# Reordering the first token-mixer stage of a two-layer diffusion backbone: an early PSUM copy, another order of gates, conditioning loads and norms

## The chip, the cores and the metric

The kernel runs on one core of one Trainium2 chip. The metric is the device time of one execution in microseconds, taken as the median of several runs. Engines are named as the profile names them: PE (TensorE, matrix products), DVE (VectorE), ACT (ScalarE), POOL (GpSimd) and SP (SyncE, which here only issues the DMA transfers). Each engine takes its own instructions in order, and waits on semaphores where it needs another engine's result.

## The reference

Two layers over 512 latent tokens of width 1024 and 256 context tokens. The first stage, which the change touches, is the pooling mixer of layer 0 up to the input of its MLP:

```python
sh1, sc1, gt1, sh2, sc2, gt2 = ada_mods(c, w_ada[i], b_ada[i])             # SiLU(c) @ w_ada + b_ada
csh1, csc1, cgt1, csh2, csc2, cgt2 = ada_mods(c_ctx, w_ada[i], b_ada[i])
h_lat = modulate(rms_norm(x, g_mix_pre[i]), sh1, sc1)                      # h * (1 + sc) + sh
h_ctx = modulate(rms_norm(ctx, g_mix_pre[i]), csh1, csc1)
y_lat = pool_mixer(h_lat, w_pool[j], pool_scale[j])
y_ctx = None if last else pool_mixer(h_ctx, w_pool[j], pool_scale[j])
x = x + gt1 * rms_norm(y_lat, g_mix_post[i])
m_lat = sq_relu_mlp(modulate(rms_norm(x, g_mlp_pre[i]), sh2, sc2), w_mlp_in[i], w_mlp_out[i])
x = x + gt2 * rms_norm(m_lat, g_mlp_post[i])
```

The context tokens take the same steps with their own vectors (`cgt1`, `csc2`, ...). Layer 1 is an attention layer with another MLP. All of it is float32; the large products are made from a high and a low part of each operand, three products for one.

## The kernel before

The 768 tokens are six tiles of 128 rows: tiles 0 to 3 are latent, 4 and 5 context. `xr` holds the residual stream, `acc` (seen as `accv[:, t, :]`) the tile that is being worked on, `hH`/`hL` (both in the buffer `ra`) the transposed input of the next product as high and low part, and `rb` the weights.

After the pooled means the stage runs, for each tile t in the order 4, 5, 0, 1, 2, 3:

- `pool_a`: 24 products of 128x256 columns into two PSUM banks (`pspool`). Tiles 4 and 5 do it early and in pieces; tile 4 has two small banks of the pool `psB` (four banks in all), the other tiles a double bank of `psA` (two double banks).
- `pool_ms`: the mean square of the mixer output, on ACT straight from PSUM (two activations with an accumulator, line 170), then two tiny POOL instructions (lines 183 and 185) that make the reciprocal root.
- `pool_b`: the mixer output times the gate row, on DVE, two halves of 512 columns (`gated`, line 326), into `acc`.
- `norm_r`: the residual add on DVE (line 329), `norm_s`: mean square of the new row on ACT and the root on POOL, `norm_c`: the scaled row into `acc`, on ACT (line 521) for every second tile and on DVE (line 523) for the others.

Then pairs of tiles (4,5), (0,1), (2,3) are transposed on PE, a quarter of the columns at a time (`turn0`, line 379, 4 transposes into `psx`), and modulated (`mod0`: two rows on ACT, line 389, and on DVE, line 391, and the split into high and low part, lines 395 and 396). The first MLP product (`Inner.part`, line 562) uses each quarter as soon as it is there.

The conditioning vectors come from 14 entries of `CONDITIONING`. Each is a load from `w_ada` (1 MB, or two for a wide entry), a small product `ada_mm` (line 227; 8 matmuls whose 32-column pieces lie side by side in the array), a DVE transpose (line 233), a small product with `sel` (line 238) and an add (line 249). The entries 6 and 7 are the mixer's gate GT1, 8 and 9 the MLP's scale SC2 and shift SH2 for the first half of the columns, 10 to 13 the same for the second half. A gate row is made from such a vector by `gate_rows` (4 matmuls into `psg`, a copy by ACT into `gate`), for latent tokens (`ci` 0) and context tokens (`ci` 1) and for two halves of the columns each.

The order of all this is a table of numbers: `st.at(z, function, ...)` enters a step at due time z, and the steps are emitted by rising z. Up to z = 47.3 (DVE and ACT) and 48 (PE) the emitted order is kept on each engine; in the rest of the stage a scheduler with a timing model of its own may reorder. Loads of `w_ada` go into four buffers in SBUF, so a load can be issued once the matmuls on the load four places ahead of it are done; all loads go through SP's one queue. The weights of the first MLP product are loaded once (`w_in(0, 0, ...)`) and split into `rb` by ACT (line 142) and DVE (line 145).

Of the kernel before, what the change touches and what calls it, by code (L numbers as in the profile page):

```python
# [22 lines left out]
TOK = LAT + CTX  # L23
# [11 lines left out]
SH1, SC1, GT1, SH2, SC2, GT2 = range(6)  # L35
# [33 lines left out]
def backbone(ctx: ExitStack, tc, x, ctx_in, w_ada, w_pool, pool_scale, w_qkv, g_q, g_k, w_o, w_mlp_in,  # L69
# [4 lines left out]
    te, ve, sc = Kept(tc, nc.tensor, ordered), Kept(tc, nc.vector, mixed), Kept(tc, nc.scalar, mixed)  # L74
# [42 lines left out]
    hH = ra[:, 0:KT * TOK].rearrange("p (k n) -> p k n", n=TOK)  # L117
    hL = ra[:, KT * TOK:].rearrange("p (k n) -> p k n", n=TOK)
    accv = acc.rearrange("p (t n) -> p t n", n=D)
# [19 lines left out]
    def split(raw, hi, lo, pin=False, q=None):  # L139
        if q is not None:  # L140
            raw, hi, lo = (z[:, 512 * q:512 * q + 512] for z in (raw, hi, lo))
        a = sc.copy(hi, raw)  # L142
        if pin:
            tc.keep_in_program_order(a)
        b = ve.tensor_tensor(out=lo, in0=raw, in1=hi, op=ALU.subtract)  # L145
        if pin:
            tc.keep_in_program_order(b)
# [177 lines left out]
    def gated(t, dst, src, n0, n1, pool=False):  # L325
        return (gp if pool else ve).tensor_tensor(out=dst[:, n0:n1], in0=src, in1=gate[:, slot[t], n0:n1], op=ALU.mult)
# [107 lines left out]
    rs, mix, yg, first = {}, {}, {}, []  # L434
# [62 lines left out]
            mean_square(pss[q], ss[:, q:q + 1])  # L497
        rs[t] = rstd(ss, 2)

    def pool_b(t):  # L500
        for q in range(2):
            gated(t, accv[:, t, :], mix[t][q], 512 * q, 512 * q + 512)

    def norm_r(t, half=False):
# [34 lines left out]
    hids0 = [(rb[:, 3072 * b:3072 * b + 1536], rb[:, 3072 * b + 1536:3072 * b + 3072]) for b in range(2)]  # L539
# [58 lines left out]
    ring = Ring(unit)  # L598
# [117 lines left out]
    def w_in(i, g, rg, pin=False, wait=None):  # L716
        return rg.load(w_mlp_in[i, g], 256, pin, wait)
# [4 lines left out]
    st = Steps()  # L722
    for t in range(NT):
        st.at(4.6 + 1.3 * t, rows_a, t)
    landing = ((19.3, 21.4, 22.4), (23.8, 25.9, 27), (27.1, 28.15, 28.7), (28.9, 30.0, 30.5), (31.4, 32.4, 33.4),
               (33.7, 34.8, 35.2), (40.6, 42.65, 43.9), (44.2, 46.25, 47.2),
               (51, 53, 53.8), (55.8, 57.8, 58.6), (60.5, 61.5, 62), (62.9, 63.9, 64.4), (65.2, 66.2, 66.7), (67.7, 68.7, 69.2))
    for zs, (m, j, w) in zip(landing, CONDITIONING):
        for z, fn, also in zip(zs, (ada_mm, ada_rows, ada_sel), ((w,), (), ())):
            st.at(z, fn, 0, m, j, *also)  # L730
# [27 lines left out]
        st.at((21.5, 23.4)[h], pool_split, h, True)  # L758
        st.at((23.4, 24.4)[h], pool_split, h, False)
    raws = []  # L760
    st.at(56.5, lambda: first.append(Inner(0, w_in(0, 0, ring, False, raws), hH, hL, hids0[0], chunks0, TOK)))
    st.at(58, lambda: split(*raws[0]))
    for h in range(2):
        for ci in range(2):
            st.at((46.2, 47.6)[h] + (0.1, 0)[ci], gate_rows, 0, GT1, ci, (h,))
    order = (4, 5, 0, 1, 2, 3)
    for z, t, g in ((30.6, 4, 0), (32.5, 4, 1), (35.4, 4, 2), (36.2, 5, 0), (36.3, 5, 1), (36.4, 5, 2), (42.6, 4, 3), (42.62, 5, 3)):
        st.at(z, pool_a, t, (g,), t == 4)
    for n, t in enumerate(order):
        b = 50.5 + 2.9 * n  # L770
        if n > 1:
            st.at((47.9, 52.6, 55.6, 58.4)[n - 2], pool_a, t)
        st.at((43.8, 44.6, 50.6, 55.6, 58.6, 61.4)[n], pool_ms, t)
        st.at(b, pool_b, t)
        st.at(b + 1.5, norm_r, t)
        st.at(b + 2.8, norm_s, t)
        st.at(b + 4, norm_c, t, n % 2 == 1)
    parts0 = lambda t, q, f: first[0].part(t, f, range(2 * q, 2 * q + 2))
    block = {(4, 0): 58, (4, 1): 59.4, (0, 0): 63.4, (0, 1): 64.7, (4, 2): 66, (0, 2): 67.3, (2, 0): 69, (2, 1): 70.2,
             (2, 2): 71.4, (4, 3): 72.6, (0, 3): 73.8, (2, 3): 75}  # L780
    for (t, q), z in block.items():
        st.at(z, turn0, t, q)
        st.at(z + 0.8, mod0, t, q)
        for f in range(2):
            st.at(z + 2.4 if q < 3 else 76.5 + 2 * f + t / 10, parts0, t, q, f)
    st.at(200, open_units)
    st.run()

# [663 lines left out]
```

## Time and profile before

| what | value |
|---|---|
| median of 3 runs | 1178.41 us (1176.73 to 1180.56) |
| the profiled execution | 1178.11 us |
| its span, first to last instruction | 1176.3 us |
| mean granted PE clock | 0.996 of full speed |
| DVE busy | 938.4 us (80%) |
| ACT busy | 635.0 us (54%) |
| POOL busy | 68.1 us (6%) |

The span is what the trace shows; the profiled execution's own time holds 1.8 us around it. A row of the timeline has its start, its length, engine, source line, operation, the tiles written and read, their shape and a count, and in brackets how long the engine stood idle before it and what ended that. Steps that keep the emitted order show the line of the recording helper, 65, in place of their own. A matmul of float32 counts twice in the timeline's count where it is made of two passes. Rows of the window view give busy time of PE, weight loads, DVE, ACT and POOL, then the granted PE clock, the share of DMA engines busy, and GB/s.

### The profile page before, as it was taken

What the parts mean: (1) busy time and instruction counts of PE and PEld (TensorE: products, weight loads), DVE (VectorE), ACT (ScalarE), POOL (GpSimd) and SP (SyncE); (2) the same over time, 40 slices, a digit from 0 to 9 for tenths busy, and PEclk for the clock granted to TensorE, in tenths of its full rate; (3) what the DMA queues carried; (4) which work ended last, traced back from release to release, by engine and by line L of the source; (5) the groups of instructions that cost most, each with busy time, mean ns of one, the idle gap of its engine ahead of it and who ended that gap; (6) DMA issues with size and microseconds to landing.
All of it is one profiled execution on the core that took longest, in us unless ns stands there. A gap on an engine that the chain in (4) does not pass through costs nothing. (4 is left out here: it accounts for less than half of the span.)

```text
span 1176.3 us, 15958 instructions
## 1 busy us (share of the span) xinstructions
PE 1145.3 (97%) x6172; PEld 989.6 (84%) x6172; DVE 938.4 (80%) x1538; ACT 635.0 (54%) x1080; POOL 68.1 (6%) x120
## 2 busy tenths in 40 slices
PE   7889999999999999999999999999899999999997
PEld 5569898899899988998887889988888888888886
DVE  4677788889988998997778599877687779778876
ACT  4576655454454435555585378862676346435522
POOL 2030000000000000000231200001100000000001
PEclk9999999999999999999999999999999999999999
DMA  9983113343433434343422101115234123304212
GB/s 369 392 319 115 50 60 143 116 157 126 143 143 143 143 122 150 115 146 112 179 72 104 41 1 37 37 72 189 98 116 170 49 95 143 108 36 144 108 35 109
DMA packets 25516, 147.32 MB, mean 125 GB/s; under 512 B 2785, under 2 KB 5217, under 8 KB 9698
## 3 DMA queue, kind: packets, MB, share of 16 engines
q1 hardware_dynamic: 25442, 146.32, 34.1%
q8 instruction: 48, 0.79, 0.3%
q14 instruction: 26, 0.21, 0.1%
HBM read 138.96 MB, written 7.34 MB: 124 GB/s over the span
## 5 line engine op out<-in xcount | busy, mean ns | idle before, releaser
L807 PE MATMUL pso<-units,rb 128*128 128x512 f32 x1152 | 278.4, 392 | 0.0
L807 PEld LDWEIGHTS pso<-units,rb 128*128 128x128 f32 x1152 | 214.8, 188 | 41.2
L273 DVE SCALAR_TENSOR_TENSOR rows<-raw,cond,rows 128x256 f32<-128x256 f32 x280 | 127.0, 478 | 2.0
L819 DVE TENSOR_TENSOR acc<-acc,pso 128x512 f32<-128x512 f32 x129 | 85.4, 676 | 42.2 <-PE pso L807 42.1
L562 PE MATMUL psin<-ra,rb 128*128 128x512 f32 (+1 forms) x432 | 104.0, 343 | 1.6 <-ACT ra L364 1.6
L911 PE MATMUL pso<-units,pairs 128*128 128x512 f32 x336 | 82.3, 389 | 0.0
L562 PE MATMUL psin<-ra 128*128 128x512 f32 x256 | 80.6, 390 | 0.0
L562 PEld LDWEIGHTS psin<-ra,rb 128*128 128x128 f32 x432 | 70.9, 193 | 11.0 <-ACT ra L364 1.9
L911 PEld LDWEIGHTS pso<-units,pairs 128*128 128x128 f32 x336 | 63.1, 188 | 13.1
L915 DVE TENSOR_TENSOR acc<-acc,pso 128x512 f32<-128x512 f32 x72 | 48.7, 682 | 28.5 <-PE pso L911 28.5
L183 POOL TENSOR_SCALAR ms<-ss 128x1 f32<-128x1 f32 x20 | 11.2, 561 | 1006.7 <-ACT junk L170 963.8
L686 PE MATMUL psin<-ra,units 128*128 128x384 f32 x336 | 65.7, 337 | 0.4 <-ACT psin L698 0.4
L686 PE MATMUL psin<-sums,units 128*128 128x384 f32 x336 | 63.9, 337 | 0.0
L686 PEld LDWEIGHTS psin<-ra,units 128*128 128x128 f32 x336 | 59.7, 188 | 3.9 <-ACT psin L698 0.9
L686 PEld LDWEIGHTS psin<-sums,units 128*128 128x128 f32 x336 | 58.9, 188 | 1.7
L145 DVE TENSOR_TENSOR units<-raw,units 128x1024 fp32r<-128x1024 f32 (+2 forms) x49 | 55.3, 1150 | 3.6 <-ACT units L142 3.5
L562 PEld LDWEIGHTS psin<-ra 128*128 128x128 f32 x256 | 48.1, 188 | 10.0
L142 ACT CAST units<-raw 128x1024 fp32r<-128x1024 f32 (+2 forms) x49 | 46.8, 995 | 14.5 <-PE pso L807 10.4
L562 PE MATMUL psin<-rb 128*128 128x512 f32 (+1 forms) x144 | 53.4, 372 | 0.2 <-DVE rb L365 0.2
L817 ACT COPY acc<-pso 128x512 f32<-128x512 f32 x48 | 27.1, 587 | 49.0 <-PE pso L807 48.5
L1054 PE MATMUL psq<-units,ra 128*128 128x512 f32 x216 | 51.6, 392 | 0.0
L562 PE MATMUL psin<-rb,ra 128*128 128x512 f32 x128 | 49.8, 389 | 0.0
(277 smaller groups left out, 2347.2 us busy)
## 6 DMA issues: line engine op xcount, KB each, us to landing
raw<-in_w_ada SPq DMA_DIRECT2D x48, 1024.0 KB, 5.0
raw<-in_w_mlp_in SPq DMA_DIRECT2D x32, 1024.0 KB, 4.9
raw<-in_w_mlp_out SPq DMA_DIRECT2D x32, 1024.0 KB, 5.4
raw<-in_w_qkv SPq DMA_DIRECT2D x6, 1024.0 KB, 4.8
spill<-xr SPq DMA_DIRECT2D x10, 512.0 KB, 6.8
xr<-spill SPq DMA_DIRECT2D x10, 512.0 KB, 6.9
raw<-in_w_o SPq DMA_DIRECT2D x4, 1024.0 KB, 4.8
xr<-in_x SPq DMA_DIRECT2D x4, 512.0 KB, 6.3
```

The source lines that it names most:

```text
L142: a = sc.copy(hi, raw)
L145: b = ve.tensor_tensor(out=lo, in0=raw, in1=hi, op=ALU.subtract)
L183: gp.tensor_scalar(out=ms[:, 0:1], in0=ss[:, parts - 1:parts], scalar1=rest, scalar2=EPS, op0=ALU.add, op1=ALU.add)
L273: ve.scalar_tensor_tensor(out=r, in0=raw[:, k, :], scalar=cond[:, k, c:c + 1], in1=r, op0=ALU.mult, op1=ALU.add)
L562: te.matmul(ps[:, bank, o:o + ln], w[:, k, fs], rhs, start=start, stop=(k == KT - 1 and n == 2), skip_group_check=len(ks) < KT)
L686: te.matmul(bank, w[k], a[k], start=start and k == 0 and m == 0, stop=stop and k == 3 and m == 2, skip_group_check=True)
L807: te.matmul(pss[h][:, 0:cols[h][1]], a[:, f, ts_], w[:, f, cols[h][0]:sum(cols[h])], start=(n == 0 and not seeded[t]), stop=(n == len(seq) ...
L817: sc.copy(d, ps)
L819: ve.tensor_tensor(out=d, in0=d, in1=ps[:, 0:w], op=ALU.add)
L911: te.matmul(ps, a, w, start=(m == 0), stop=(m == len(seq) - 1))
L915: ve.tensor_tensor(out=M[n][:, t], in0=M[n][:, t], in1=ps, op=ALU.add)
L1054: te.matmul(ps, a[:, k, sl], w[:, k % 4, :], start=(k == 0 and n == 0), stop=(k == KT - 1 and n == 2))
```

## The change

```diff
+    def pool_c(t):
         for q in range(2):
+            sc.copy(accv[:, t, 512 * q:512 * q + 512], mix[t][q])
+            mix[t][q] = accv[:, t, 512 * q:512 * q + 512]
+
+    def pool_b(t, qs=range(2)):
+        for q in qs:
             gated(t, accv[:, t, :], mix[t][q], 512 * q, 512 * q + 512)
...
     landing = (...
-               (51, 53, 53.8), (55.8, 57.8, 58.6), (60.5, 61.5, 62), ...
+               (47.75, 48.5, 49.5), (52.8, 53.2, 54.7), (60.5, 61.5, 62), ...
...
-    st.at(56.5, lambda: first.append(Inner(0, w_in(0, 0, ring, False, raws), hH, hL, hids0[0], chunks0, TOK)))
-    st.at(58, lambda: split(*raws[0]))
+    st.at(62.95, lambda: first.append(Inner(0, w_in(0, 0, ring, False, raws), hH, hL, hids0[0], chunks0, TOK)))
+    st.at(63.2, lambda: split(*raws[0]))
     for h in range(2):
         for ci in range(2):
-            st.at((46.2, 47.6)[h] + (0.1, 0)[ci], gate_rows, 0, GT1, ci, (h,))
+            st.at(((47.65, 46.2), (47.7, 47.6))[h][ci], gate_rows, 0, GT1, ci, (h,))
...
+    st.at(43.9, pool_c, 4)
     for n, t in enumerate(order):
         b = 50.5 + 2.9 * n
...
-        st.at((43.8, 44.6, 50.6, 55.6, 58.6, 61.4)[n], pool_ms, t)
-        st.at(b, pool_b, t)
-        st.at(b + 1.5, norm_r, t)
-        st.at(b + 2.8, norm_s, t)
-        st.at(b + 4, norm_c, t, n % 2 == 1)
+            st.at(b, pool_b, t)
+            st.at(b + 1.5, norm_r, t)
+        else:
+            for q in range(2):
+                st.at(50.5 + 0.1 * n + 1.2 * q * (1 + n), pool_b, t, (q,))
+            st.at((51.8, 53)[n], norm_r, t)
+        st.at((43.8, 44.6, 54.8, 58, 60.5, 62.8)[n], pool_ms, t)
+        st.at((53, 54)[n] if n < 2 else b + 2.8, norm_s, t)
+        st.at((54.4, 54.6)[n] if n < 2 else b + 4, norm_c, t, n % 2 == 1)
...
-            st.at(z + 2.4 if q < 3 else 76.5 + 2 * f + t / 10, parts0, t, q, f)
+            st.at(max(z + 2.4, 63.4 + q / 10) if q < 3 else 76.5 + 2 * f + t / 10, parts0, t, q, f)
```

The first group of edits: `pool_c` lets ACT copy tile 4's mixer output out of its two PSUM banks into `acc`, and the gate product of tile 4 then reads that copy. The gate rows are made in the order context half 0, context half 1, latent half 0, latent half 1 (before: context and latent of half 0, then of half 1). The gate products of tiles 4 and 5 are entered one half at a time, and their norms earlier. The second: the MLP's scale and shift for the first half of the columns are entered earlier, the load and split of the first MLP weights later, and the mean squares of tiles 0 to 3 later.

What this does on the engines, first on PE around the gates and the first two latent tiles (`psada<-raw,cond` is `ada_mm`, `psada<-work,sel` the small product behind it, `psg` a gate row, `pspool` a mixer tile, `psx` a transpose). Before:

```order
L65 MATMUL psada<-raw,cond 32x512 x8
L65 MATMUL psg<-ident,gc 128x128 x8
L65 MATMUL psada<-work,sel 32x2x4 x4
L65 MATMUL psg<-ident,gc 128x128 x8
L65 MATMUL pspool<-rb,ra 128x256 x24
L227 MATMUL psada<-raw,cond 32x512 x8
L490 MATMUL pspool<-rb,ra 128x256 x24
L227 MATMUL psada<-raw,cond 32x512
L490 MATMUL pspool<-rb,ra 128x256 x6
L238 MATMUL psada<-work,sel 32x2x4 x4
L490 MATMUL pspool<-rb,ra 128x256 x18
L227 MATMUL psada<-raw,cond 32x512 x7
```

With the change, from the same first row:

```order
L65 MATMUL psada<-raw,cond 32x512 x8
L65 MATMUL psg<-ident,gc 128x128 x4
L65 MATMUL psada<-work,sel 32x2x4 x4
L65 MATMUL psg<-ident,gc 128x128 x12
L65 MATMUL psada<-raw,cond 32x512 x8
L65 MATMUL pspool<-rb,ra 128x256 x24
L490 MATMUL pspool<-rb,ra 128x256 x8
L238 MATMUL psada<-work,sel 32x2x4 x4
L490 MATMUL pspool<-rb,ra 128x256 x16
L227 MATMUL psada<-raw,cond 32x512 x8
L379 MATMUL psx<-ident,acc 128x128 x8
L490 MATMUL pspool<-rb,ra 128x256 x24
```

The vector of the second gate half is made after one gate row, not after two; the first MLP vector stands ahead of tile 0 and is whole, where the second one stood split, one matmul ahead of tile 2 and seven behind it; eight transposes of tiles 4 and 5 stand ahead of tile 2.

A little later on PE, behind tile 2, with the change (`psin` is the first MLP product; the transposes and MLP rows of the stage's rest follow in both kernels in other interleavings):

```order
L227 MATMUL psada<-raw,cond 32x256
L490 MATMUL pspool<-rb,ra 128x256 x5
L238 MATMUL psada<-work,sel 32x2x4 x4
L490 MATMUL pspool<-rb,ra 128x256 x19
L227 MATMUL psada<-raw,cond 32x256 x15
L379 MATMUL psx<-ident,acc 128x128 x2
L238 MATMUL psada<-rows,sel 32x2x2 x8
L379 MATMUL psx<-ident,acc 128x128 x6
L567 MATMUL psin<-ra,rb 128x256
L227 MATMUL psada<-raw,cond 32x256 x8
```

Here a single matmul of a narrow vector (256 columns) stands ahead of tile 3, and the other fifteen of two vectors behind it. From the second MLP product on (`psin<-ra,units`, 96 matmuls) PE's order is the same in both kernels but for one matmul of the next piece.

On ACT, over the stage's middle, from the mean square of tile 0's mixer output on (`junk` rows are mean squares, from `pspool` of the mixer output and from `xr` of a tile's new row; `L142` is the split of the MLP weights; `L521`, with the change `L526`, the scaled row; `L389` the modulation of a transposed quarter). Before:

```order
L170 ACTIVATE junk,ss<-pspool 128x512 x2
L170 ACTIVATE junk,ss<-xr 128x1024
L170 ACTIVATE junk,ss<-pspool 128x512
L142 CAST rb<-raw 128x2048
L170 ACTIVATE junk,ss<-pspool 128x512
L170 ACTIVATE junk,ss<-xr 128x1024
L170 ACTIVATE junk,ss<-pspool 128x512 x2
L521 ACTIVATE acc<-xr,rs 128x1024
L170 ACTIVATE junk,ss<-xr 128x1024
L170 ACTIVATE junk,ss<-pspool 128x512 x2
L170 ACTIVATE junk,ss<-xr 128x1024
L389 ACTIVATE acc<-psx,mods_91,avec_94 128x2x128 x2
```

With the change:

```order
L170 ACTIVATE junk,ss<-xr 128x1024 x2
L170 ACTIVATE junk,ss<-pspool 128x512
L526 ACTIVATE acc<-xr,rs 128x1024
L170 ACTIVATE junk,ss<-pspool 128x512 x3
L170 ACTIVATE junk,ss<-xr 128x1024
L170 ACTIVATE junk,ss<-pspool 128x512 x2
L170 ACTIVATE junk,ss<-xr 128x1024
L389 ACTIVATE acc<-psx,mods_91,avec_94 128x2x128 x2
L142 CAST rb<-raw 128x2048
L526 ACTIVATE acc<-xr,rs 128x1024
L170 ACTIVATE junk,ss<-pspool 128x512
L395 CAST ra<-acc 128x4x128 x2
```

`L142` stood between the two mean squares of tile 1 and now stands behind the first two `L389`, ahead of tile 3's mean squares (the last `pspool` row); tile 5's mean squares of the new row stand ahead of tile 0's mixer output. Ahead of this piece, the two `pool_c` copies stand before tile 5's mean squares. On SP the only change in the queue is that the load of the first MLP weights goes behind the two loads of entries 10 and 11.

More of the change, by code (lines that the diff above doesn't have):

```diff
@@ L498, in pool_ms @@
         rs[t] = rstd(ss, 2)
-    def pool_b(t):
+    def pool_c(t):
         for q in range(2):
+            sc.copy(accv[:, t, 512 * q:512 * q + 512], mix[t][q])
+            mix[t][q] = accv[:, t, 512 * q:512 * q + 512]
+    def pool_b(t, qs=range(2)):
+        for q in qs:
             gated(t, accv[:, t, :], mix[t][q], 512 * q, 512 * q + 512)
@@ L726, in backbone @@
                (33.7, 34.8, 35.2), (40.6, 42.65, 43.9), (44.2, 46.25, 47.2),
-               (51, 53, 53.8), (55.8, 57.8, 58.6), (60.5, 61.5, 62), (62.9, 63.9, 64.4), (65.2, 66.2, 66.7), (67.7, 68.7, 69.2))
+               (47.75, 48.5, 49.5), (52.8, 53.2, 54.7), (60.5, 61.5, 62), (62.9, 63.9, 64.4), (65.2, 66.2, 66.7), (67.7, 68.7, 69.2))
     for zs, (m, j, w) in zip(landing, CONDITIONING):
```

## The prediction

> **What bounds the kernel now.** I read the window view first: where PE has idle time, and where its clock falls. Columns: start and end, length, busy time with count of PE, weight loads, DVE, ACT and POOL, granted PE clock, DMA share, GB/s.
>
> ```profile
> 35.00:41.00 6.00, 3.46 (x55) 1.86 (x44) 4.76 (x13) 1.71 (x4) 0.00 (x0) 1.00 1.01 415
> 73.00:83.00 10.00, 7.01 (x77) 4.16 (x76) 8.34 (x17) 9.04 (x18) 4.74 (x9) 0.83 0.97 364
> 76.00:79.00 3.00, 0.95 (x14) 0.43 (x10) 2.72 (x7) 3.00 (x7) 1.61 (x4) 0.99 0.84 262
> 79.00:82.00 3.00, 2.48 (x18) 1.69 (x22) 2.35 (x6) 3.00 (x7) 1.47 (x4) 0.50 1.02 419
> 83.00:105.00 22.00, 22.00 (x204) 20.92 (x203) 14.61 (x28) 12.46 (x23) 0.00 (x0) 1.00 0.45 175
> 105.00:200.00 95.00, 95.00 (x484) 86.60 (x483) 72.54 (x116) 55.38 (x82) 0.00 (x0) 1.00 0.23 85
> ```
>
> From 83 us on PE is busy all the time, to 200 and beyond, and its order from the second MLP product on is the same in both kernels. So the whole effect is one number: by how much earlier PE reaches that product (105.39 us before). Between 73 and 83 PE works 7.01 of 10 us, at a mean clock of 0.83; in 76 to 79 ACT is busy throughout. The view of waits for PE, 47 to 106 us, names what holds it (total, times, longest):
>
> ```profile
> PE psx L379 <- ACT acc L521: 1.4, 1, 1.4
> PE psx L379 <- DVE acc L391: 1.2, 1, 1.2
> PE psg L65 <- ACT gate L65: 0.7, 1, 0.7
> PE psg L65 <- DVE gc L292: 0.5, 1, 0.5
> PE psada L227 <- DVE mods L249: 0.4, 1, 0.4
> ```
>
> Two waits lie at the gate rows (1.2 us), three between 74 and 80 us (3.0 us). The timeline of PE gives their places and the durations that I use:
>
> ```profile
> 49.29 1.16 PE L65 MATMUL psg<-ident,gc 128*128 128x128 f32 x8
> 52.95 2.05 PE L65 MATMUL psg<-ident,gc 128*128 128x128 f32 x16 [0.48 <-DVE gc L292]
> 54.76 3.11 PE L65 MATMUL pspool<-rb,ra 128*128 128x256 f32 x24
> 57.80 1.92 PE L227 MATMUL psada<-raw,cond 128*32 128x512 f32 x16
> 59.65 3.13 PE L490 MATMUL pspool<-rb,ra 128*128 128x256 f32 x24
> 62.71 1.04 PE L227 MATMUL psada<-raw,cond 128*32 128x512 f32 x2
> 63.69 0.98 PE L490 MATMUL pspool<-rb,ra 128*128 128x256 f32 x6
> 67.12 1.92 PE L227 MATMUL psada<-raw,cond 128*32 128x512 f32 x14
> 68.97 0.44 PE L379 MATMUL psx<-ident,acc 128*128 128x128 f32 x2
> 69.34 1.07 PE L227 MATMUL psada<-raw,cond 128*32 128x256 f32 x16
> 77.57 0.33 PE L379 MATMUL psx<-ident,acc 128*128 128x128 f32 x1 [1.19 <-DVE acc L391]
> 79.52 1.54 PE L379 MATMUL psx<-ident,acc 128*128 128x128 f32 x6 [1.35 <-ACT acc L521]
> 80.99 1.73 PE L227 MATMUL psada<-raw,cond 128*32 128x256 f32 x16
> 82.65 0.66 PE L379 MATMUL psx<-ident,acc 128*128 128x128 f32 x4
> 92.33 1.47 PE L379 MATMUL psx<-ident,acc 128*128 128x128 f32 x12
> 96.68 8.87 PE L562 MATMUL psin<-ra,rb 128*128 128x256 f32 x72
> 105.39 0.86 PE L562 MATMUL psin<-ra,units 128*128 128x384 f32 x4
> ```
>
> Taken from start to start: a mixer tile 3.04 us (54.76 to 57.80), a wide vector 1.85, eight matmuls of a narrow one 1.00, a transpose 0.12 (1.47 / 12), an MLP matmul 0.121 (8.71 / 72). One wide matmul alone costs 0.98 (62.71 to 63.69), and the seven left over still 1.85.
>
> **Gates: 1.1 us.** Before, the second gate row waits for ACT's copy of the first, and the last pair for the vector `gc`, whose small product stands behind two rows. Now one row stands ahead of that product, and tile 4's two banks are free early. One row and the product end at 50.45; the transposed vector is ready on DVE as before, and its add gives `gc` at about 50.9; three rows at 0.9 (1.81 for the two from 52.95) end at 53.65. The wide vector, now first, ends at 55.5 and tile 0 at 58.5. Before, the same two were through at 59.65: 1.1 gained.
>
> `pool_c` adds two ACT copies out of PSUM; the nearest row is the copy of a gate row:
>
> ```profile
> 50.49 0.58 ACT L65 COPY gate<-psg 128x512 f32<-128x512 f32 x1 [1.53 <-PE psg L65]
> ```
>
> At 0.58 each they push tile 5's mean squares back by 1.2, and ACT stood idle for 1.53 us ahead of 50.49: some 0.3 of cover is left. Without the cover they would cost up to 1.2, all of it ahead of the first gate copy; a gain is possible too, since tile 4's gate product reads a copy in place of PSUM, but DVE has room there. I take nothing for them. The half-wise gate products are the same four instructions, earlier.
>
> **Vectors: 0.5 us.** The second wide vector is no longer split (2.83 before, 1.85 now: 0.98 gained), but one narrow matmul stands alone ahead of tile 3 (0.5, half of the wide one's 0.98 by its half width) and fifteen behind it (2.0), where two narrow vectors at 1.00 would do: 0.5 lost. Between nothing gained (if the rest pays as the seven did) and 1.0 I take 0.5.
>
> **Stalls: 1.0 us.** The durations on DVE and ACT, by groups of the same shape, 47 to 106 us (busy, mean ns, idle before):
>
> ```profile
> L326 DVE TENSOR_TENSOR acc<-pspool,gate 128x512 f32<-128x512 f32 x12 | 7.7, 682 | 4.0 <-ACT gate L305 1.8 <-ACT junk L170 1.3 <-ACT gate L65 0.9
> L329 DVE SCALAR_TENSOR_TENSOR xr<-acc,rs,xr 128x1024 f32<-128x1024 f32 x6 | 7.4, 1261 | 0.0
> L391 DVE TENSOR_SCALAR acc<-psx,avec,mods 128x256 f32<-128x256 f32 x12 | 6.1, 538 | 4.5 <-ACT acc L389 4.5
> L145 DVE TENSOR_TENSOR rb<-raw,rb 128x2048 fp32r<-128x2048 f32 x1 | 2.3, 2293 | 0.1
> L142 ACT CAST rb<-raw 128x2048 fp32r<-128x2048 f32 x1 | 1.9, 1891 | 0.0
> L170 ACT ACTIVATE junk<-xr 128x1024 bf16<-128x1024 f32 x6 | 6.3, 1054 | 0.1
> L170 ACT ACTIVATE junk<-pspool 128x512 bf16<-128x512 f32 x8 | 4.8, 597 | 7.1 <-PE pspool L490 4.7 <-PE pspool L65 2.4
> L389 ACT ACTIVATE acc<-psx,mods,avec 128x256 f32<-128x256 f32 x12 | 6.1, 559 | 4.8 <-PE psx L379 4.7
> ```
>
> PE after 58.5: tile 1 with its small product to 61.85, the second wide vector to 63.7, eight transposes to 64.65, tile 2 to 67.7, the lone matmul to 68.2, tile 3 with a small product to 71.4, the fifteen to 73.4. No input is late there by the groups: the context gates are copied by some 52.4 (51.8 for the second row, 0.58 for the copy), four L326 and two L329 take 5.2 us from there, and a square, a root and a scaled row some 3 more: 61, and the transposes come at 63.7.
>
> ACT, from tile 2's end at 67.8: two mean squares (0.60 each, and some 0.1 for the read-out of each) to 69.3, tile 1's `xr` square to 70.35, two L389 to 71.35, the cast L142 to 73.2, L526 to 74.3. DVE: tile 2's gate products from 69.3 to 70.5, L329 to 71.65, two L391 to 72.6, two narrow transposes and small vectors to 73.9, the split L145 to 76.15. The first MLP product needs L145. PE has eight transposes and four small products to do between 73.4 and then, some 1.4 us, so it stands still for 1.5. A second wait of about 0.5 follows at 82.75, behind L396 and L391 of the next quarters. The sum is 2.0 against 3.0 before.
>
> **Clock: 1.4 us.** Before, the six transposes and the narrow vector took from 79.52 to 82.65, 3.13, where 6 x 0.12 and 1.00 make 1.7: the clock was 0.50 there, right after 3 us with 0.95 of work. With 3.46 busy of 6 us (35 to 41) it stayed at 1.00. The changed stretch, 73.4 to 76.4, has about 1.4 of 3 busy: nearer to the second case, so I take no fall. The bound on the other side is the same 1.4 lost again. [...]
>
> **Sum.** 1.1 + 0.5 + 1.0 + 1.4 = 4.0 us. The walk itself, carried on: at 76.2 one MLP matmul of 144, a narrow vector, and so on; from 83.3 there are 118 MLP matmuls and 24 transposes left, 118 x 0.121 + 24 x 0.12 = 17.2, so the second MLP product starts at 100.5 to 101, 4.4 to 4.9 earlier; the difference is in changes between kinds of matmul, which single transposes pay before. I take 4.2, near the terms, since a chain of some eighteen steps on DVE from 69 to 83 us has hand-overs that I have not priced. The profiled execution took 1178.11 us (0.3 below the median): **1173.9**. From the bounds: 4.9 gained gives 1173.2, 2.7 gained 1175.4; with 0.8 to either side for the spread of single runs the forecast's own range is 1172.4 to 1175.4.
>
> **Rivals.** *The clock falls again* (0.12). For it: 1.5 us of standing still in a 3 us stretch, on a gate that has let go after 0.95 of 3. Against it: the row of 35 to 41 us. Gain 4.2 - 1.4 = 2.8: 1175.3.
>
> *The gain is lost downstream* (0.08). DVE works 72.54 of 95 us from 105 to 200, and more densely at first; if PE came 4 us earlier and its results waited for banks that DVE must empty, part of it would be given back. Against it: what DVE does there is set off by PE's own results, and moves with them. Half lost: 1176.0.
>
> *The reorder doesn't reach PE* (0.06). The stalls may only change their place: if L396 and L145, late by 2 us on a DVE at 8.34 of 10, hold PE as long as L391 and L521 did, only gates and vectors remain, 1.6 less 0.4 for hand-overs: 1176.9.
>
> *Slower: ACT waits for the MLP weights* (0.14). The load of the first MLP weights now stands behind two more loads in SP's queue, and ACT's cast stands ahead of tile 1's scaled row and tile 3's mean squares, so everything behind it on ACT, and through DVE all of PE, waits if it is late.
>
> ```profile
> raw<-in_w_mlp_in SPq DMA_DIRECT2D x1, 1024.0 KB, 11.3
> 49.80 0.43 SPq L123 DMA_DIRECT2D raw<-in_w_mlp_in  x1
> 69.47 0.42 SPq L123 DMA_DIRECT2D raw<-in_w_mlp_in  x1
> ```
>
> Before, it was issued at 49.80 and landed 11.3 us later, at 61.1. Behind two more loads of 1 MB, at the 2.5 us each that 415 GB/s give, it would land at 66.1; I let the loads ahead of it be issued at about 55.5, when the first wide vector has freed a buffer. ACT asks for it at 71.35: 5.2 us of room. From 75.5 on the gain is gone. If it were issued only when the other MLP load was before, 69.47, and took 10 us, ACT would stand 8.3 us late and the time would be 1182. For it: SP issues strictly in order, and its DMA was at 0.97 of its share from 73 to 83. Against it: the room.
>
> **How the numbers follow.** The forecast has 0.60; the rivals 0.12, 0.08, 0.06, 0.14. A measurement of this kernel tells about 0.3%, or 3.5 us, from no change, so faster needs less than 1174.9. The forecast's own spread puts five sixths of it there (0.50), the clock rival and the lost gain a third and a fifth (0.06): 0.56. The slower case reaches past 1181.9 in half of its share, with something for what I have not thought of: 0.12. The rest, 0.32, lies within 0.3%. Range: 1172.4, the forecast's low end, to 1178.4, which takes in all cases but the slower one.
>
> **What would show it.** Right: tile 0's 24 matmuls start at about 55.5 (54.76 before, but now with the wide vector done); tile 3's last at 71.4; a wait of PE for L145 at about 76; clock 1.00 in 76 to 82; the first 128x384 product at 100.5 to 101.5, and everything behind it earlier by the same amount. The gate term falls if a `psg` group still waits for ACT; `pool_c` costs if the first gate copy starts after 50.5. Wrong altogether: a DMA wait of L142 on ACT near 71; a clock of 0.50 between 74 and 83; stalls that add up to 3 us or more; or PE waits behind 105 us that before does not have.

## The result, and the profile after

The changed kernel takes **1173.64 us** (median of 7 runs, 1172.66 to 1176.41), the kernel before 1178.41 (7 runs): a ratio of 0.9962, with a 95% interval of 0.9950 to 0.9974. The forecast was 1173.9. The profiled execution took 1173.48, with a span of 1171.7 (before: 1178.11 and 1176.3).

The window view of the changed kernel, at the places that were shown of before (PE, weight loads, DVE, ACT, POOL, granted PE clock, DMA share, GB/s):

```profile
73.00:83.00 10.00, 9.17 (x108) 6.82 (x107) 9.61 (x18) 9.25 (x17) 3.37 (x6) 1.00 0.69 240
76.00:79.00 3.00, 2.17 (x32) 1.46 (x33) 2.86 (x5) 3.00 (x8) 0.04 (x1) 1.00 0.99 404
79.00:82.00 3.00, 3.00 (x34) 2.42 (x33) 3.00 (x7) 2.42 (x6) 2.54 (x4) 1.00 0.39 154
105.00:200.00 95.00, 95.00 (x480) 86.22 (x479) 73.35 (x119) 55.16 (x82) 0.00 (x0) 1.00 0.24 84
```

PE works 9.17 of 10 us where it worked 7.01, its clock stays at 1.00, and behind 105 us it still never stands still. Its waits from 47 to 106 us are two in place of five:

```profile
PE psada L227 <- DVE mods L249: 0.7, 1, 0.7
PE psg L65 <- DVE gc L292: 0.6, 1, 0.6
```

The timeline of PE:

```profile
51.51 1.16 PE L65 MATMUL psg<-ident,gc 128*128 128x128 f32 x8
53.42 2.92 PE L65 MATMUL psg<-ident,gc 128*128 128x128 f32 x24 [0.58 <-DVE gc L292]
56.27 1.92 PE L65 MATMUL psada<-raw,cond 128*32 128x512 f32 x16
61.09 1.12 PE L490 MATMUL pspool<-rb,ra 128*128 128x256 f32 x8
...
64.42 1.92 PE L227 MATMUL psada<-raw,cond 128*32 128x512 f32 x16
66.28 1.09 PE L379 MATMUL psx<-ident,acc 128*128 128x128 f32 x8
...
70.17 0.62 PE L227 MATMUL psada<-raw,cond 128*32 128x256 f32 x2
70.71 0.86 PE L490 MATMUL pspool<-rb,ra 128*128 128x256 f32 x5
...
74.15 1.93 PE L227 MATMUL psada<-raw,cond 128*32 128x256 f32 x30
76.01 0.44 PE L379 MATMUL psx<-ident,acc 128*128 128x128 f32 x2
...
77.81 0.38 PE L567 MATMUL psin<-ra,rb 128*128 128x256 f32 x1
78.89 1.07 PE L227 MATMUL psada<-raw,cond 128*32 128x256 f32 x16 [0.69 <-DVE mods L249]
...
102.87 3.46 PE L567 MATMUL psin<-ra,units 128*128 128x384 f32 x19
```

From the first gate row to the second MLP product it is 102.87 - 51.51 = 51.36 us, where before had 105.39 - 49.29 = 56.10: **4.74 us less**. But the first gate row itself starts 2.22 us later, though PE's order ahead of it is the same. The timeline and the window view of the changed kernel around 41 us show why:

```profile
40.70 5.46 PE L65 MATMUL pspool<-rb,ra 128*128 128x256 f32 x24 [0.83 <-DVE mods L65]
```

```profile
41.00:44.00 3.00, 3.00 (x15) 3.00 (x15) 1.21 (x3) 2.79 (x6) 0.00 (x0) 0.50 0.98 407
```

The 24 matmuls took 3.10 before; here the clock was at 0.50. The span's difference is made up of four parts: +2.22 up to the first gate row, -4.74 in the changed stretch, -0.61 from there to a matmul of layer 1's first MLP product (the one that waits for DVE's low part: 842.30 - 105.39 = 736.91 before, 839.17 - 102.87 = 736.30 after; a wait of 0.36 for ACT at 625 us, which only before has, is part of it), and -1.5 behind that, where before runs at half clock from 843.6 to 847.0 us and the changed kernel does not. Together -4.6. So the profile alone doesn't settle what is the change's doing.

### The profile page after: what moved, and what is told of

Its sections match the earlier page's. It is cut to its first block, busy times and chain, and to the rows that moved or that the text cites. A ratio compares the mean times of both kernels' runs of the same rounds, so it can differ in the third digit from the quotient of the medians.

```text
span 1171.7 us, 15966 instructions
## 1 busy us (share of the span) xinstructions
PE 1143.0 (98%) x6172; PEld 989.2 (84%) x6172; DVE 938.4 (80%) x1538; ACT 636.7 (54%) x1082; POOL 67.0 (6%) x120
## 4 chain that ended last, share of the span: by engine, by line
PE 49%; issue 42%; POOL 3%; DVE 2%; ACT 2%; DMA 1%; SPq 0%; POOLq 0%; DVEq 0%; ACTq 0%
PE pso L817 22%; PE psin L691 18%; PE psin L567 3%; PE psq L1064 2%; PE pspool L65 1%; POOL rs L185 1%; PE psada L65 1%; PE pspool L490 1%; POOL rs L1073 1%; DMA raw<-in_w_ada 1%; DMA xr<-in_x 1%; PE psada L227 1%; POOL ms L183 1%; DVE ra L65 0%; ACT junk L170 0%
## 5 line engine op out<-in xcount | busy, mean ns | idle before, releaser
L145 DVE TENSOR_TENSOR units<-raw,units 128x1024 fp32r<-128x1024 f32 (+2 forms) x49 | 55.1, 1148 | 4.5 <-ACT units L142 4.4
L142 ACT CAST units<-raw 128x1024 fp32r<-128x1024 f32 (+2 forms) x49 | 46.8, 994 | 14.0 <-PE pso L817 10.2
```

## The experiments

For each run but the first of the kernel with extra matmuls (below): the length from first gate row to second MLP product (called the stretch below), PE's busy time and mean granted clock from 73 to 83 us of its profile, and the median time.

| kernel | stretch | PE busy, 73 to 83 | clock there | time (runs) |
|---|---|---|---|---|
| before | 56.10 | 7.01 | 0.83 | 1178.41 (7) |
| before_again | 56.34 | 7.01 | 0.97 | 1179.06 (1) |
| early_squares | 56.09 | 7.31 | 0.83 | 1177.6 (1) |
| gates_alone | 55.91 | 6.84 | 0.66 | 1177.63 (12) |
| keep_warm_again | 53.76 | 8.29 | 0.83 | 1174.07 (4) |
| mlp_alone | 53.61 | 8.58 | 0.83 | 1175.04 (12) |
| late_vectors | 51.81 | 8.89 | 1.00 | 1174.58 (1) |
| early_weights | 51.40 | 9.97 | 1.00 | 1173.98 (1) |
| after | 51.36 | 9.17 | 1.00 | 1173.64 (7) |
| after_again | 51.36 | 9.17 | 1.00 | 1173.59 (5) |
| no_copy | 51.36 | 9.17 | 1.00 | 1173.42 (6) |
| quarters_no_copy | 51.15 | 9.41 | 1.00 | 1173.14 (5) |
| split_quarters | 51.13 | 9.42 | 1.00 | 1172.53 (6) |

The first gate row comes between 48.90 and 53.20 us in these profiles, so 73 to 83 us is not quite the same work in each. Taken from 23.7 to 33.7 us behind the first gate row, PE's busy time differs from the third column by 0.14 at most, and every clock that is below 1.00 in the fourth column stays so.

The mean granted clock of a whole run tells how much of it ran at half clock: the profiles with one fall of 3.4 us have 0.997 or 0.998, those with 6.8 us 0.996, the one with 10.2 us 0.995. At the same 0.996, eighteen runs of before take 1177.8 to 1179.2 us and five of the changed kernel 1173.5 to 1174.2, so a gain of about 4.4 is there without a difference in falls.

### Both kernels once more

No edit.

> The changed kernel once more, nothing altered. In its first profile PE takes 51.36 us from the first gate row (51.51) to the second MLP product (102.87), against 56.10 before; but PE's clock fell to 0.50 in 41 to 44, in work that the change does not touch, and tile 4's and 5's 24 matmuls there took 5.46 us where before they took 3.10. Theory A (the fall at 41 is a matter of chance): the stretch from first gate row to second MLP product is again 51.0 to 51.8; the 24 matmuls take 3.1 in some profiles and about 5.4 in others, whichever kernel. Theory B (the change brings the fall): 5.4 again, and in every profile of a kernel with this change. The median is within 0.2% of the first one's, 1173.6.

> The kernel before once more, nothing altered. Theory A (falls of the clock are a matter of chance, by where the stalls lie against windows that run on their own): the falls seen in its first profile, 0.50 in 79 to 82 and again near 838, need not come again, and one at 41 may come; where the clock holds in 79 to 82 the stretch from first gate row to second MLP product is 54.7 in place of 56.10. Rival (stalls as long as those of 74 to 80 always bring the fall): 56.1 again, to 0.1.

The second profile of the changed kernel, its timeline of PE:

```profile
40.73 3.10 PE L65 MATMUL pspool<-rb,ra 128*128 128x256 f32 x24 [0.87 <-DVE mods L65]
```

The 24 matmuls take 3.10, the first gate row starts at 49.15, and the stretch is 51.36 again, to the hundredth. The fall at 41 is not the change's: theory A holds for it, B falls. This time the clock fell from 837.4 to 840.8 us, at the same place in the work as before's second fall. The second profile of before also starts its first gate row 2.2 us late, at 51.48: in work that is the same in all these kernels, a DMA wait is 0.9 us longer there and the clock falls from 27.7 to 31.2 us.

The second profile of before has the same five waits with the same lengths, but the clock holds up to 82 us. Its window view behind that:

```profile
82.00:83.00 1.00, 1.00 (x10) 0.56 (x12) 1.00 (x2) 1.00 (x2) 0.00 (x0) 0.68 1.02 418
83.00:84.00 1.00, 1.00 (x16) 0.40 (x8) 0.59 (x2) 1.00 (x4) 0.61 (x2) 0.50 1.05 430
84.00:85.00 1.00, 1.00 (x11) 0.51 (x4) 1.00 (x3) 1.00 (x3) 0.18 (x1) 0.50 1.00 406
85.00:86.00 1.00, 1.00 (x7) 1.00 (x6) 0.71 (x2) 1.00 (x2) 0.00 (x0) 0.62 1.06 426
```

The fall came later, 82.4 to 85.8, and cost as much: 56.34. PE was busy for 2.88 of the 3.4 us of the fall in the first profile and for all 3.40 in the second; at the clock of 0.50 half of that, 1.4 and 1.7, estimates the cost, and leaves 54.7 and 54.6 for the stretch without it. So here the rival was right in substance: the long stalls bring the fall in both profiles, and only its place moves. The table's third column orders all kernels by it: in all six profiles with 8.58 us or less of work in 73 to 83 the clock falls in or right behind the stalls, in all seven with 8.89 or more it doesn't. That is one or two profiles of each kernel, and near that border it is not certain, as the second group below shows.

### Each group of edits alone

First group alone (copy, gate order, halves, norms of tiles 4 and 5), against the changed kernel:

```diff
-               (47.75, 48.5, 49.5), (52.8, 53.2, 54.7), (60.5, 61.5, 62), ...
+               (51, 53, 53.8), (55.8, 57.8, 58.6), (60.5, 61.5, 62), ...
-    st.at(62.95, lambda: first.append(...
-    st.at(63.2, lambda: split(*raws[0]))
+    st.at(56.5, lambda: first.append(...
+    st.at(58, lambda: split(*raws[0]))
-        st.at((43.8, 44.6, 54.8, 58, 60.5, 62.8)[n], pool_ms, t)
+        st.at((43.8, 44.6, 50.6, 55.6, 58.6, 61.4)[n], pool_ms, t)
-            st.at(max(z + 2.4, 63.4 + q / 10) if q < 3 else ...
+            st.at(z + 2.4 if q < 3 else ...
```

> Only the first group: the copy of tile 4, the order of gate rows, gate products by halves, norms of tiles 4 and 5 early; vectors, MLP weights and mean squares are entered as before. Theory M (the second group removes the stalls at 74 to 80 and with them the clock's fall): first gate row to second MLP product 55.3 us, 0.8 less than the 56.10 before; waits for L391 and L521 of 2 to 3 us remain, the clock falls or nearly so; time 0.05 to 0.1% under before. Rival G (the first group does, since tiles 4 and 5 are ready early and can be transposed ahead of tile 2): about 52.0, waits under 1 us, time 0.3% under before.

Second group alone: the same five lines the other way, on the kernel before.

> Only the second group: vectors of the MLP earlier, load and split of its weights later, mean squares later; gate rows in the old order and no copy of tile 4. Theory M: first gate row to second MLP product 51.9 us (56.10 less 0.6 for the unsplit vector, 2.3 for stalls, 1.4 for the clock), gate waits of 0.7 and 0.5 as before; time 0.3% under before. Rival G: about 55.5 (0.6 less), waits of 2 to 3 us for L391 and L521 or their like, time within 0.1% of before.

The first group alone, waits of PE and the window view:

```profile
PE psx L379 <- ACT acc L526: 2.0, 1, 2.0
PE psada L238 <- DVE mods L249: 1.2, 1, 1.2
```

```profile
76.00:79.00 3.00, 1.32 (x6) 1.32 (x7) 2.60 (x6) 3.00 (x6) 1.49 (x3) 0.50 0.92 337
79.00:82.00 3.00, 3.00 (x29) 1.34 (x27) 1.86 (x5) 2.98 (x6) 0.57 (x1) 0.50 1.03 422
```

The gates' gain is there (tile 0's first matmul comes 4.58 us after the first gate row, 5.47 before), but the later waits are 3.2 us and the clock is halved for 6.8 us (75.9 to 82.8): of 0.9 us, 0.19 is left, and the time is 0.9994 of before (0.9985 to 1.0003). Theory M fits better than rival G, which is refuted.

The second group alone has 53.61, between both theories' numbers, and 0.9977 (0.9965 to 0.9989). One wait of 1.4 us for L521 is left, with this window view:

```profile
76.00:79.00 3.00, 1.58 (x22) 0.77 (x16) 3.00 (x4) 3.00 (x7) 0.27 (x1) 1.00 0.97 393
79.00:82.00 3.00, 3.00 (x20) 2.53 (x20) 2.98 (x9) 2.54 (x7) 2.12 (x4) 0.50 0.53 210
```

The gains of the parts don't add: 0.19 and 2.49 alone, 4.74 together. The half clock, which before and both parts pay and the whole doesn't, is by the estimate above worth 1.4 us in before and 1.7 in the second group alone (3.40 us of work in its fall), so it can be most of the missing 2.06; this was not measured apart. Nor is the fall certain for the second group alone: its twelve runs go from 1172.35 us at a mean clock of 0.999, which leaves no room for a fall of 3.4 us and is faster than any of the changed kernel's twelve runs (the fastest: 1172.64), to 1179.16 at 0.992.

### Which edit does it

The changed kernel without the call of `pool_c`:

```diff
-    st.at(43.9, pool_c, 4)
```

> The changed kernel without the copy of tile 4: its gate products read PSUM; every other instruction stands in the same order on PE. Theory C (the copy frees two of the four small banks for the gate rows): the second to fourth gate row wait for banks or for ACT's copies, 0.7 to 2.0 us more ahead of tile 0, and the stretch to the second MLP product is 52.0 to 53.4. Rival (four banks are enough, the new order alone frees the rows): 51.36 as with the copy, within 0.3, and ACT has 1.06 us less to do ahead of the first gate copy.

51.36 again: the copy, named first in the change, is worth nothing. The four small banks are enough; what is left of the first group on PE ahead of tile 0 is the order of the gate rows, and it frees PE of the wait for ACT. (That order was not tried by itself.) Theory C falls.

The wide vectors at their old times:

```diff
-               (47.75, 48.5, 49.5), (52.8, 53.2, 54.7), (60.5, 61.5, 62), ...
+               (51, 53, 53.8), (55.8, 57.8, 58.6), (60.5, 61.5, 62), ...
```

> The changed kernel with the two wide vectors of the MLP entered at the old times (51 and 55.8 in place of 47.75 and 52.8). Theory V (the vectors' early place is what lets PE go on: modulation of tiles 4 and 5 and the unsplit vector): first gate row to second MLP product 53 to 55, with waits of 1 to 3 us for the modulated rows. Rival W (the late weights and mean squares free ACT, the vectors give only the 0.6 of the unsplit matmuls): 51.9 to 52.2.

51.81: 0.45 more, and the clock holds. Theory V falls, and rival W has it nearly to the number. But not all of the 0.45 need be the unsplit matmuls: behind the gates PE waits for 1.0 us here (L396, L233 and L391), where the changed kernel waits for 0.7.

The MLP weights at their old times (the three lines of `first`, `split` and `parts0` above):

> The changed kernel with the load and the split of the first MLP weights (and the MLP rows that follow from them) at their old times; the cast L142 then stands on ACT ahead of tile 1's square and of the first two L389. Theory W1 (the late cast frees ACT, and that removes most of the stalls): first gate row to second MLP product 52.3 to 53.5, waits of 1 to 2 us for L389, L391 or L526. Rival W2 (the place of the cast is indifferent, ACT has room): 51.2 to 51.8.

51.40: rival W2. Here PE even works 9.97 of 10 us from 73 to 83, and its longest wait comes just ahead of the second product (timeline of PE):

```profile
101.71 8.59 PE L567 MATMUL psin<-ra,units 128*128 128x384 f32 x48 [0.93 <-ACT work L574]
```

It waits for ACT, which empties the bank of the first product. Moving the weights back gains 0.9 us and loses it there.

The mean squares of tiles 0 to 3 at their old times:

```diff
-        st.at((43.8, 44.6, 54.8, 58, 60.5, 62.8)[n], pool_ms, t)
+        st.at((43.8, 44.6, 50.6, 55.6, 58.6, 61.4)[n], pool_ms, t)
```

> The changed kernel with the mean squares of tiles 0 to 3 entered at their old times (50.6 to 61.4 in place of 54.8 to 62.8); the scheduler then puts tile 0's squares ahead of tile 5's new row and the first L389 behind the cast. Theory S1 (the order of the squares against the norms of tiles 4 and 5 removes the stalls): 52.3 to 53.5 from first gate row to second MLP product. Rival S2 (indifferent): 51.2 to 51.8.

56.09, far beyond S1's numbers: undoing this one line gives the whole gain back, with a fall of the clock again (78.3 to 81.7). Its waits of PE and the row of the longest:

```profile
PE psin L567 <- DVE ra L396: 3.0, 4, 2.3
PE psin L567 <- ACT ra L395: 0.8, 1, 0.8
```

```profile
78.15 1.56 PE L567 MATMUL psin<-ra,rb 128*128 128x256 f32 x6 [2.34 <-DVE ra L396]
```

With the old times tile 0's squares stand ahead of those of tiles 4's and 5's new rows on ACT, the first transposes fall behind tile 2, and when PE has begun the first MLP product, L396 stands behind the split L145 on DVE and PE has nothing else to do. Which of these shifts weighs how much was not taken apart. So the late squares are needed, but with gates_alone and mlp_alone in view they aren't enough: mlp_alone has them and keeps 2.25 us of the loss. The squares alone on the kernel before were not tried.

### Two attempts at more

The split in quarters, with the adds of the narrow vectors ahead of the last two on DVE:

```diff
-    st.at(63.2, lambda: split(*raws[0]))
+    for n, z in enumerate((63.2, 63.3, 64.6, 64.7)):
+        st.at(z, lambda n: split(*raws[0], q=n, pinb=n > 1), n)
...
+        if (i, j) == (0, 2) and m in (SC2, SH2):
+            tc.keep_in_program_order(z)
```

> The changed kernel with the split of the MLP weights in four quarters of 512 columns, the adds of the two narrow vectors (L249) ahead of the last two quarters on DVE. In the changed kernel PE's only wait behind the gates is 0.69 us for these adds, which stand behind the whole split L145 of 2.25 us. Theory (that order alone makes the wait): it is gone, first gate row to second MLP product 50.6 to 50.9 (51.36 less 0.5 to 0.7), median 0.5 us less. Rival (DVE has no room, 9.6 of 10 us busy there, so another wait comes in its place): 51.2 to 51.8, and a wait for L398 (the low part) or L145.

The wait for L249 is gone, and two others are there (waits of PE):

```profile
PE psg L65 <- DVE gc L294: 0.6, 1, 0.6
PE psx L381 <- ACT acc L528: 0.4, 1, 0.4
PE psin L569 <- DVE acc L328: 0.2, 1, 0.2
```

51.13, the rival, a little better than it said: of 0.69 us, 0.23 is gained. The time, 0.9945 of before (0.9925 to 0.9964), lies below the changed kernel's, but the intervals overlap, and falls of the clock make the difference: three of the six runs have a mean clock of 0.999 and take 1171.1 to 1171.3, the other three have 0.996 and take 1173.7 to 1174.1, no less than the changed kernel at 0.996. Without the copy as well:

> Split of the MLP weights in quarters, as before, and without the copy of tile 4. If the copy is worth nothing, the stretch is the 51.13 of the quarters with the copy, to 0.05, and the median within 0.1% of the quarters' 1172.5; if it frees something there, 51.3 or more.

51.15, so the copy is worth nothing there either; 0.9957 (0.9943 to 0.9970).

Last, extra matmuls in the waits ahead of 41 us:

```diff
+    def warm(dst, n):
+        for _ in range(n):
+            te.matmul(dst, hH[:, 0, 4 * P:5 * P], wp3H[:, 0, :], start=True, stop=True)
...
+        if (i, m, j) == (0, SH1, 3):
+            warm(ps[:, 256:512], 4)
...
+        if i == 0 and j == 3 and m in (SC1, SH1):
+            warm(ps[:, 256:512], 2 if m == SC1 else 7)
...
+    st.at(32.49, lambda: warm(mix[4][0][:, 256:512], 6))
```

> The changed kernel with 19 extra matmuls of 128x256 (0.12 us each, 2.3 us together) put where PE waits between 36 and 41 us, ahead of the stretch in which the clock fell in one of its two profiles; they write columns of PSUM that nobody reads. Theory A: PEclk is 1.00 from 35 to 47 in the profile, the 24 matmuls of tiles 4 and 5 take 3.1, the first gate row starts by 49.4, and since the fall of 2.2 us no longer comes in any run, the median is about 1 us under the changed kernel's (1172.2 to 1173.2). Rival (the extra matmuls don't fit the waits): first gate row after 49.6, median 1174 or more. The scheduler also moves a few transposes of the later stage, so the stretch from first gate row to second MLP product is taken from the profile by itself.

> The kernel with the 19 extra matmuls once more: its first profile fell into an execution of 2938 us. In the seven other runs the mean granted clock was 0.997 to 0.999, against 0.995 to 0.998 for the changed kernel, yet the median was 1173.9 and no gain. Theory A: clock 1.00 from 35 to 47, first gate row by 49.4, and the stretch to the second MLP product is 1 to 2 us longer than 51.36 because the scheduler moved transposes. Rival (the extra matmuls themselves lengthen the way): first gate row at 50 or later, stretch 51.4.

The first profile is of an execution of 2938 us, in which all of PE was slower (the costliest matmuls take 828 ns where the changed kernel's take 392, at a granted clock of 1.00); why is open, and that execution is left out. The second profile, timeline and waits of PE:

```profile
41.89 3.11 PE L65 MATMUL pspool<-rb,ra 128*128 128x256 f32 x24
50.32 1.16 PE L65 MATMUL psg<-ident,gc 128*128 128x128 f32 x8
```

```profile
PE psada L227 <- DVE mods L257: 1.7, 1, 1.7
```

The clock holds at 1.00 from 24 to 47, as theory A has it, and in all eleven other runs the mean clock is 0.997 to 0.999. But the extra matmuls delay the 24 by 1.16 us (41.89 against 40.73), and the scheduler's new order of the later steps costs 2.4 us of the stretch, a clock fall at 79 among it. Nothing is gained: medians of 1173.6 (seven runs) and 1174.1 (four), and even the seven runs at 0.999 take 1173.1 to 1174.2. Both theories had a part of it.

## Why the prediction was right, point by point

- **The whole.** Everything rested on how much earlier PE gets to the second MLP product, counted from the first gate row: 4.2 was taken, between 4.0 by terms and 4.4 to 4.9 by the walk; 4.74 was measured, in both profiles of the changed kernel. The walk was the better sum: it had the product at 100.5 to 101, and in the second profile, where the first gate row starts at 49.15 against 49.29 before, it is at 100.51. The medians differ by 4.8.
- **Luck in the number.** 1173.9 lies 0.3 from the median measured, closer than its parts. The 4.2 is 0.5 short, and was taken from the profiled execution, 0.3 below the median before. The gates were 0.3 too high and the stalls 1.3 too low. The forecast's own range has 0.8 for the spread at its low end only (at its high end it would be 1176.2).
- **Gates, 1.1.** Mis-sized: the vector and tile 0 behind the gates end 9.58 us after the first gate row (61.09 - 51.51), 10.36 before (59.65 - 49.29): 0.78. PE is through with the first row and the small product after 1.33 us (53.42 - 0.58 - 51.51), where 1.16 was taken, the wait for `gc` is 0.58 where 0.45 was reckoned, and three rows take 2.85, not 2.75. Pricing the copy at nothing was right (no_copy).
- **Vectors, 0.5.** 1.86 whole, 0.54 for the lone narrow one, 1.86 for the fifteen: 4.26 against 4.83, 0.57. late_vectors gives 0.45.
- **Stalls, 1.0.** The step that failed: 3.0 went to 0.7, not to 2.0, so 2.3 in place of 1.0. The prediction has PE stand still for 1.5 (1.35 by its own figures) until L145 is done, because, as it says, "The first MLP product needs L145". The timelines of ACT and DVE in the changed kernel:

```profile
73.73 1.90 ACT L142 CAST rb<-raw 128x2048 fp32r<-128x2048 f32 x1
```

```profile
76.51 2.25 DVE L145 TENSOR_TENSOR rb<-raw,rb 128x2048 fp32r<-128x2048 f32 x1
78.68 0.22 DVE L249 TENSOR_TENSOR mods<-psada,vec 128x4 f32<-128x4 f32 x2
```

  Counted from the first gate row, L145 ends at 27.25 us, where 26.86 was reckoned, so that end was nearly right. But PE comes to the MLP product only at 26.30, not at 25.5: it is 0.4 late by the end of the fifteen, from the gates, and the eight transposes and the small products take 1.80 (76.01 to 77.81), not 1.4. So 0.4 of what this stall lost is work in its place, and no gain. And the first MLP matmul starts at 77.81, in the middle of L145: it reads the high part, which the cast has written. What then waits is a narrow vector, 0.69 us, for the adds L249 that stand behind L145 on DVE. The second stall, 0.5 at 82.75, did not come.
- **Clock, 1.4.** Right in size, but not for the reason given: 1.00 from 73 to 83 in every profile of the changed kernel. The row of 35 to 41 us, which was to show that half-busy work keeps the clock, was a matter of chance: in the first profile of the changed kernel the clock fell at 39.4, in the same work. And with 1.58 of 3 us busy, a little more than the 1.4 of the forecast, it fell in mlp_alone. With the stall as forecast the rival of a second fall was thus likelier than 0.12; the clock held because the stall was shorter. That the fall would come from the length of the stalls is borne out by the table.
- **The terms** measured, 0.78 + 0.57 + 2.3 + 1.4, are 5.0, 0.3 more than the stretch shows. Which changes between kinds of matmul hold that remains open.
- **Rivals.** The clock did not fall again. Nothing was lost downstream: 736.3 us from there to layer 1 against 736.9. The weights came in time, with the room that was reckoned. The queue of SP in the changed kernel:

```profile
58.63 0.42 SPq L123 DMA_DIRECT2D raw<-in_w_mlp_in  x1
```

  Issued at 58.63, the load landed 9.9 us later (DMA view of 58.6 to 58.7 us), at 68.5; the cast starts at 73.73: 5.2 us of room. From the first gate row on, landing and cast are at 17.0 and 22.2 us, where 16.8 and 22.1 were forecast.
- **What the prediction left out:** the clock also falls by chance outside the changed stretch (between 24 and 47 us in 8 of the 12 profiles without extra matmuls), and whether it falls in half-busy work is partly chance as well. That the profiled execution came out at 1173.48 is the sum of a larger gain, a loss of 2.2 near 41 us, and 1.5 saved near 843.

## What to carry to other kernels

Measure a change to one stage from an anchor ahead of it to an anchor behind it: the stretch came out at 51.36 in both profiles of the changed kernel and within 0.24 us in the two of before, while whole executions of one kernel differ by 4 to 6 us (1176.4 to 1182.8 for before). Where a scheduler works from due times, undo the edits one by one: the copy that gave the change its name was worth nothing, and a line that moved four mean squares could not be spared. And count a stall twice, once for its length and once for the clock that it may halve behind it (0.50 for 3.4 us here, an estimated 1.4 of the 56.10); parts that each leave the stall too long don't show what they are worth alone.

## What the runs showed of the hardware

The clock falls to 0.50 for 3.4 us or for twice that: 79.0 to 82.4 and 82.4 to 85.8 in the two profiles of before, 39.4 to 46.2 in the first one of the changed kernel. The place relative to a stall differs from run to run. In the four profiles with two falls within 60 us of each other, their starts, worked out from the mean clock of 1 us windows, lie apart by whole multiples of 3.41 us: 13.66, four times, in quarters_no_copy (27.38 and 41.04); 37.56, eleven times, in mlp_alone (41.46 and 79.02) and in early_squares (40.72 and 78.28); 54.62, sixteen times, in before_again (27.74 and 82.36). PE was not idle ahead of every fall: in mlp_alone it was busy for 1.58 us of the 3 (76 to 79). Unchanged work took part in this by chance: in the stretch with DMA and DVE waits from 24 to 47 us the clock fell in 8 of the 12 profiles without extra matmuls, and near 840 us in 4 of the 12. Near 41 us this costs up to 2.4 us (5.46 against 3.10), half of what the change gains.
